# Down-projection of a gated MLP with tokens on partitions: weights as the moving operand, two Strassen lots of 16 K tiles, and the final norm along the free axis

## The chip, the cores and the metric

The kernel runs on one core of one Trainium2 chip. Its time is the device time of one execution in microseconds (us). Before the change three runs took 2834.66, 2835.13 and 2835.55 us.

## The reference

One layer of a decoder on x of 512 tokens by 2048 features (`S`, `D`), all in float32. Six vectors of 2048 (shift, scale and gate, twice) come from a conditioning vector c. The change touches the end:

```python
mod = silu(c) @ w_ada + b_ada
sh1, sc1, gt1, sh2, sc2, gt2 = split(mod, 6)
h = rmsnorm(x, g_mix) * (1 + sc1) + sh1
x = x + (1 + gt1) * mixer(h, positions, w_in, w_a, w_b, w_o)
h = rmsnorm(x, g_ffn) * (1 + sc2) + sh2
u = conv_b + causal depthwise convolution of width 3 of (h @ w_up)
a, b = split(u, 2)
x = x + (1 + gt2) * ((silu(a) * b) @ w_down)          # w_down: 5632 x 2048
out = rmsnorm(x, g_final)
```

`rmsnorm(x, g)` divides each token by the root of its mean square over the 2048 features and multiplies by g.

## The kernel before, in words

Features lie on partitions and the 512 tokens along the free axis nearly everywhere: an activation is a list of tiles of 128 features by 512 tokens, and 2048 features are 16 of them (`KT`), 5632 are 44 (`NJ`). A K tile is 128 rows of a weight matrix.

**Three products for one.** Every float32 operand is split into a high and a low part that TensorE takes in its fp32r format (`parts` and `prep` for weights: `wh` on ACT, L132, `wl` on DVE, L134; `split` for activations: L161 and L163). `mm3` (L140 to L144) issues three matmuls: high by high (L142), high by low (L143), low by high (L144). The operand named first stands in the array, the second moves.

**Strassen units.** `unit` multiplies n K-tile pairs of a weight matrix by an activation with seven products of half size instead of eight. Its matmuls move half of the tokens, 256 columns. DVE forms sums of weight quarters (L232, L236, L270, L274) and of the products (L240, L272, L273, L276, L278). A unit with 16 K tiles makes 168 matmuls and two output tiles. w_x (32 units, 64 output tiles, loop at L635), w_o (8 units, L1047) and w_up use it. A unit calls `between` twice, after its second and fourth product, and there other work is put into the queues. In w_x that is the next step of `beside()` (rope tables, rope of the indexer's operands), and one `ada` half at the second call (`some_ada`).

**Ada halves.** `ada_half` (L295) loads 128 rows by 1024 columns of w_ada (512 KB) and lets DVE multiply by silu(c) and sum along the row (L298). The numbers t = 0 to 95 stand for the 96 tiles of the six vectors. The gate of the MLP is t = 80 to 95.

**Down-projection (from L1168).** `yd` in DRAM holds silu(a) * b, two K tiles to a tile. `group` runs six plain K tiles over all 16 output tiles: 288 matmuls of 512 columns, sums to `sumd` in DRAM. Then eight Strassen units over the next 16 K tiles (loop at L1229), each with 168 matmuls of 256 columns; the sums are added to `sumd` and saved to `sume`. Then `group` runs the last 22 K tiles: for each output tile 66 matmuls of 512 columns, and in the last tile 132 of 256 columns, one half of the tokens after the other. With each output tile come two `ada` halves (`prepare`, L1246), the load of x1 (the residual, kept in `x1d`), the load of `sume`, and on DVE the sum with them (L1243, L1244). ACT squares the tile (L984) and POOL adds up the squares (L986).

**Final norm.** The squares lie along partitions, so `rms` (L338) sums them with matmuls against ones, takes root and reciprocal (L348, L349), and spreads the result over the partitions with two more matmuls (L355). DVE (L1287) and POOL (L1285) multiply the 16 tiles by it and g_final, and eight transfers of 512 KB bring them out, L1289. The second half of the tokens does this after the last matmul.

**w_o.** Each of the first seven units adds x (`residual`), saves x1 to `x1d`, squares it and adds the squares up with an accumulate DMA on POOL (L1062).

**Order and queues.** A tile scheduler places the instructions by priority; within an engine they run in the written-out row, and a waiting instruction holds all behind it on its engine. Loads of weights, of `ada` and the outputs go through SP's queue, loads and saves of activations and all accumulate DMAs through POOL's. Tiles with a tag share a small set of buffers (`raw` has 8, `wh` and `wl` 3 each).

Of the kernel before, what the change touches and what calls it, by code (L numbers as in the profile page):

```python
# [10 lines left out]
F32 = mybir.dt.float32  # L11
# [7 lines left out]
P = 128  # L19
# [12 lines left out]
FIRST = 6  # L32
MID = 16
LAST = NJ - FIRST - MID
# [41 lines left out]
def block_kernel(ctx: ExitStack, tc: tile.TileContext, A: dict, out: bass.AP):  # L76
# [36 lines left out]
    vec = sb.tile([P, 96 + 3 * KT], F32, tag="vec", name="vec")  # L113
    nc.scalar.dma_start(vec, A["vecs"])
    b_ada = vec[:, :96]
    g_mix, g_ffn, g_fin = (vec[:, 96 + i * KT : 96 + (i + 1) * KT] for i in range(3))
# [168 lines left out]

    def c_silu():
        cb = []
        for half in range(2):
            c = t2k("raw", 8, w=1024)
            nc.sync.dma_start(c, A["c"][:, half * 1024 : (half + 1) * 1024].to_broadcast([P, 1024]))  # L290
            act(c, c, AF.Silu)
            cb.append(c)
        return cb
# [324 lines left out]
    ada_left = [(t, half) for t in range(32, 80) for half in range(2)]  # L618
# [359 lines left out]
    x1d = [dr.tile([P, S], F32, tag=f"x1d{j}", name=f"x1d{j}") for j in range(KT)]  # L978
    x1 = []

    def squares(x, j, done):

        sq = t2k("T", 2) if j == 0 else t2k("w", 2)
        act(sq, x, AF.Square)  # L984
        if 0 < j < KT - 1:
            nc.gpsimd.tensor_tensor(done[0], done[0], sq, ALU.add)  # L986
        else:
            done.append(sq)

    def between(i, *pins):  # L990
        with behind(*pins):
            if i:
                some_ada()
# [53 lines left out]
    for u in range(KT // 2):  # L1047
# [6 lines left out]
        for i, c in enumerate(unit(A["w_o"][u], f, between, late)):  # L1054
            j = 2 * u + i
            if not late:
                residual(c, j, xr[i])
                nc.gpsimd.dma_start(x1d[j], c)
                sq = t2k("T", 2) if j == 0 else both[:, i * S : (i + 1) * S]
# [5 lines left out]
        if u == KT // 2 - 2:  # L1065
            some_ada(len(ada_left))
            ada_end(48, 80)
# [94 lines left out]
    for j in range(NU, NJ):  # L1162
        if j < 2 * NU:
            finish(j - NU, *ups[2 * (j - NU) : 2 * (j - NU) + 2])
        finish(j, *unit(A["w_up"][j - NU], f))


    def group(src, first, n, stop, done):  # L1168

        chunks = [(c, min(8, n - c)) for c in range(0, n, 8)]  # L1170

        def weights(j):
            return [prep(src[j, :, c * P : (c + m) * P], m * P) for c, m in chunks]

        y = []
        ps = acc(), att()
        for c, m in chunks:
            w = [prep(src[j, :, c * P : (c + m) * P], m * P) for j in range(2)]
            for k in range(c, c + m, 2):
                at = yd[(first + k) // 2]  # L1180
# [201 lines left out]
```

## Time and profile before

| what | before |
|---|---|
| three runs, median | 2835.13 us |
| profiled execution, time | 2834.82 us |
| profiled execution, span | 2832.7 us |
| mean granted clock of TensorE, share of full | 0.996 |
| PE busy | 2785.6 us, 98% |
| DVE, ACT, POOL busy | 84%, 49%, 9% |
| moved by DMA | 510.81 MB |

The span runs from the first instruction to the last; the time includes what lies around it. Busy times are sums of instructions that did work, waits not included. The stage in question is the last sixth, from 2338.8 us. The rows that go with it stand below, ahead of the prediction.

### The profile page before, as it was taken

The numbers are of one execution on the slowest core, as the hardware profiler recorded it, in microseconds if no ns is written. First come the engines' busy times: TensorE is split into PE (matmuls) and PEld (weight loads), VectorE is DVE, ScalarE is ACT, GpSimd is POOL, SyncE is SP. The second block draws the span as 40 slices with busy tenths as digits, with TensorE's granted clock in tenths as the row PEclk, the third lists the DMA queues.
The fourth block names the chain that finished last, engine by engine and source line by source line (L and its number), as shares of the span: only waits on it lengthen the run. The fifth ranks groups of instructions, "written<-read, shape, count | busy, mean of one in ns | idle before, by whom it ended". The sixth has DMA issues, their size and how long they took to land.

```text
span 2832.7 us, 49071 instructions
## 1 busy us (share of the span) xinstructions
PE 2785.6 (98%) x19562; PEld 2589.8 (91%) x19562; DVE 2387.5 (84%) x3446; ACT 1383.6 (49%) x1951; POOL 261.5 (9%) x452
## 2 busy tenths in 40 slices
PE   9999999999999999999999999999999999999997
PEld 6779999999998768889999999999999998998886
DVE  8979888988897899788888988888888887886554
ACT  5544444455556665434466554545454555444221
POOL 0100000000002111111110000000000001010111
PEclk9999999999999999999999999999999999999999
DMA  9964456555566458766552333333333346448663
GB/s 358 335 224 148 159 180 206 203 172 177 182 210 213 153 169 304 251 203 206 181 188 101 125 114 123 114 126 110 127 109 127 109 138 232 162 150 287 218 191 128
DMA packets 151880, 510.81 MB, mean 180 GB/s; under 512 B 19474, under 2 KB 23954, under 8 KB 151652
## 3 DMA queue, kind: packets, MB, share of 16 engines
q1 hardware_dynamic: 116836, 397.47, 41.9%
q0 software_dynamic: 34368, 109.83, 11.3%
q8 instruction: 153, 2.51, 0.4%
q14 instruction: 75, 0.61, 0.1%
q10 hardware_dynamic: 448, 0.39, 0.0%
HBM read 443.74 MB, written 60.46 MB: 178 GB/s over the span
## 4 chain that ended last, share of the span: by engine, by line
PE 82%; DVE 9%; issue 5%; DMA 2%; ACT 1%; POOL 0%; DVEq 0%; ACTq 0%; POOLq 0%
PE acc L144 13%; PE acc L142 13%; PE acc L143 13%; PE att L144 13%; PE att L142 13%; PE att L143 13%; DVE raw L298 2%; DVE wl L134 2%; DVE F L163 1%; DMA raw<-in_w_va 1%; PE acc L714 1%; PE acc L808 1%; ACT wh L132 1%; PE acc L776 0%; PE outs L914 0%
## 5 line engine op out<-in xcount | busy, mean ns | idle before, releaser
L132 ACT ACTIVATE wh<-raw 128x1024 fp32r<-128x1024 f32 (+2 forms) x787 | 820.3, 1044 | 1164.0 <-PE acc L143 299.0
L134 DVE TENSOR_TENSOR wl<-raw,wh 128x1024 fp32r<-128x1024 f32 (+2 forms) x787 | 943.3, 1201 | 151.6 <-ACT wh L132 140.8
L142 PE MATMUL acc<-F,wh 128*128 128x256 f32 (+1 forms) x2996 | 890.5, 299 | 6.8 <-ACT F L161 5.0
L144 PE MATMUL acc<-F,wl 128*128 128x256 f32 (+1 forms) x2996 | 894.6, 299 | 1.7 <-DVE wl L134 1.6
L143 PE MATMUL acc<-F,wh 128*128 128x256 f32 (+1 forms) x2996 | 895.5, 299 | 0.1
L144 PE MATMUL att<-F,wl 128*128 128x256 f32 (+1 forms) x2858 | 852.3, 298 | 3.0 <-DVE wl L134 3.0
L143 PE MATMUL att<-F,wh 128*128 128x256 f32 (+1 forms) x2858 | 852.7, 298 | 1.2 <-DVE F L163 1.2
L142 PE MATMUL att<-F,wh 128*128 128x256 f32 (+1 forms) x2858 | 848.8, 299 | 5.0 <-ACT wh L132 4.6
L142 PEld LDWEIGHTS acc<-F,wh 128*128 128x128 f32 x2996 | 572.9, 191 | 27.6 <-ACT F L161 6.8
L143 PEld LDWEIGHTS acc<-F,wh 128*128 128x128 f32 x2996 | 573.3, 191 | 20.4 <-DVE F L163 2.3
L144 PEld LDWEIGHTS acc<-F,wl 128*128 128x128 f32 x2996 | 573.1, 191 | 20.0 <-DVE wl L134 2.5
L142 PEld LDWEIGHTS att<-F,wh 128*128 128x128 f32 x2858 | 547.6, 192 | 23.5 <-ACT wh L132 5.8
L143 PEld LDWEIGHTS att<-F,wh 128*128 128x128 f32 x2858 | 547.8, 192 | 19.9 <-DVE F L163 4.3
L144 PEld LDWEIGHTS att<-F,wl 128*128 128x128 f32 x2858 | 547.4, 192 | 19.8 <-DVE wl L134 4.5
L298 DVE SCALAR_TENSOR_TENSOR raw<-raw,raw 128x1024 f32<-128x1024 f32 x186 | 227.0, 1228 | 71.1 <-DMA raw<-in_w_ada 63.1
L232 DVE TENSOR_TENSOR raw<-raw,raw 128x1024 f32<-128x1024 f32 x89 | 108.5, 1219 | 13.3 <-DMA raw<-in_w_x 9.1
L236 DVE TENSOR_TENSOR raw<-raw,raw 128x1024 f32<-128x1024 f32 x89 | 108.7, 1221 | 1.4
L274 DVE TENSOR_TENSOR raw<-raw,raw 128x1024 f32<-128x1024 f32 x88 | 107.5, 1221 | 1.5
L270 DVE TENSOR_TENSOR raw<-raw,raw 128x1024 f32<-128x1024 f32 x88 | 107.1, 1217 | 0.1
L1088 POOL DMA_DIRECT2D yd<-w x44 | 23.8, 540 | 871.7 <-DVE w L1087 830.0
L142 PE MATMUL att<-wh,F 128*128 128x512 f32 x192 | 78.3, 408 | 0.0
L144 PE MATMUL att<-wh,F 128*128 128x512 f32 x192 | 75.3, 392 | 0.0
(301 smaller groups left out, 2664.0 us busy)
## 6 DMA issues: line engine op xcount, KB each, us to landing
raw<-in_w_ada SPq DMA_DIRECT2D x186, 512.0 KB, 4.9
raw<-in_w_up SPq DMA_DIRECT2D x164, 512.0 KB, 3.3
raw<-in_w_x SPq DMA_DIRECT2D x128, 512.0 KB, 4.0
raw<-in_w_down SPq DMA_DIRECT2D x64, 512.0 KB, 4.4
xd<-F POOLq DMA_DIRECT2D x64, 256.0 KB, 3.0
F<-xd POOLq DMA_DIRECT2D x64, 256.0 KB, 4.5
raw<-in_w_o SPq DMA_DIRECT2D x32, 512.0 KB, 4.0
raw<-in_w_down SPq DMA_DIRECT2D x32, 384.0 KB, 4.1
```

The source lines that it names most:

```text
L132: act(wh, raw, AF.Copy)
L134: tt(wl, raw, wh.bitcast(F32), ALU.subtract)
L142: mm(ps, ah, bh, start=first, stop=False, skip_group_check=not check)
L143: mm(ps, ah, bl, start=False, stop=False, skip_group_check=not check)
L144: return mm(ps, al, bh, start=False, stop=last, skip_group_check=not check)
L163: tt(lo, src, hi.bitcast(F32), ALU.subtract)
L232: last_v = tt(s, a21, a22, ALU.add)
L236: tt(s, s, a11, ALU.subtract)
L270: tt(a11, a11, a21, ALU.subtract)
L274: tt(a12, a12, s, ALU.subtract)
L298: stt(raw, raw, 1.0, cb[half], ALU.mult, ALU.mult, accum_out=macc[:, t, half : half + 1])
L714: mm(dots[:, :W], both[:, b * P : (b + 1) * P], kiR[i][:, :W], start=i == 0, stop=i == 1)
```

## The change

**Layout.** In the down-projection, tokens now lie on partitions and the output features along the free axis. The split activation (128 K rows by 128 tokens) stands in the array, and weights move, 512 output features at a time. There are 16 output blocks (t, b): 128 tokens by 512 features. The 44 K tiles become 6 plain, 16 Strassen, 2 plain, 16 Strassen, 4 plain (`AT`). A Strassen lot pairs the K tiles, token halves and feature halves; it runs in two halves v of 1024 features, each four groups of K tiles times seven products of 12 matmuls, 336 of 512 columns.

**Sums.** Plain and first-lot blocks go to `sumd` in DRAM, by accumulate DMAs on POOL (`add_to`). In the second lot `base_of` takes each block, adds `sumd` to it by an accumulate DMA into SBUF, multiplies by the gate row on DVE (L1307 of the new code), and adds x1, token-major, by another accumulate DMA. The last four K tiles are multiplied by the gate row and added to that.

**Moved.** x1 is turned on PE in the w_o stage (`turn`, 4 transposes per tile, an ACT copy and a save to `x1t`; the last tiles within the first w_up units). The 32 `ada` halves of the gate go into units 16 to 31 of w_x, two more per unit. The gate row is saved to DRAM as one row, 2,048 elements of 4 bytes each, and loaded as a broadcast.

**Removed.** The reload of x1, the matmuls of the final `rms`, POOL's sums of squares, and `c_silu`. The final norm squares along the free axis with a sum in the same ACT instruction, has four groups of tokens, and 16 output transfers of 256 KB. The output has shape (4, 128, 2048) on the device.

```diff
+D0, D1, D2 = 6, 2, 4
+AT = [0, D0, D0 + MID, D0 + MID + D1, D0 + 2 * MID + D1]
...
-    ada_left = [(t, half) for t in range(32, 80) for half in range(2)]
+    ada_left = [(t, half) for t in range(32, 96) for half in range(2)]
...
             with behind(*pins):
                 next(work)
-                if i:
+                if i or u >= 16:
+                    some_ada()
+                if i and u >= 16:
                     some_ada()
...
+    def turn():
+
+        if to_turn:
+            j, x = to_turn.pop(0)
+            ps = outs()
+            for b in range(NQB):
+                nc.tensor.transpose(ps[:, b * P : (b + 1) * P], x[:, b * P : (b + 1) * P], ident)
+            o = slot()
+            act(o, ps, AF.Copy)
+            save(x1t[:, :, j * P : (j + 1) * P], o.rearrange("p (b f) -> p b f", b=NQB))
...
+            save(gate_row.rearrange("o (t p) -> p (o t)", p=P), gates)
...
+    add_to = lambda o, i: nc.gpsimd.dma_start(o, i, accum_op=ALU.add)
...
+                for i in range(2):
+                    k = 2 * c + i
+                    for t in range(NQB):
+                        mm3(ps[t], cols(y[k], t), cols(w, i, S), k == 0, k == n - 1)
...
+    def strassen_down(v, src, f, done, step=lambda i: None):
+
+        r1, rb = [att() for _ in range(2)], [att() for _ in range(2)]
+        ra, rc = [acc() for _ in range(2)], [acc(), outs()]
+        groups = range(len(f) // 2)
+
+        def product(ps, raw, name, g, first):
+            w = parts(raw)
+            for k in range(2):
+                for i in range(2):
+                    mm3(ps[i], cols(f[2 * g + k][name], i), cols(w, k, S), first and g + k == 0,
+                        g == groups[-1] and k == 1, check=False)
+
+        kept = []
+        for g in groups:
+            a11, a21, a22 = (load(src[g, q]) for q in (0, 2, 3))
+            product(r1, a11, "B11", g, True)
+            tt(a21, a11, a21, ALU.subtract)
+            product(ra, a21, "T3", g, True)
+            tt(a22, a22, a21, ALU.subtract)
+            product(rb, a22, "T2", g, True)
+            tt(a11, a22, a11, ALU.add)
+            product(rc, a11, "T1", g, True)
+            kept.append(a22)
+            step(g)
...
+        for i in range(2):
+            c22.append(slot())
+            tt(c22[i], rc[i], x[i], ALU.add)
+        for i in range(2):
+            tt(c22[i], c22[i], e3[i], ALU.add)
+            done((2 + i, 2 * v + 1), c22[i])
+        for g in groups:
+            a12, a22 = (load(src[g, q]) for q in (1, 3))
+            product(r1, a12, "B21", g, False)
+            product(ra, a22, "T4", g, False)
+            tt(a12, a12, kept[g], ALU.subtract)
+            product(rc, a12, "B22", g, False)
+            step(len(groups) + g)
...
+    def base_of(tb, c):
+        t, b = tb
+        add_to(c, sumd[tb])
+        tt(c, c, row[b], ALU.mult)
+        add_to(c, x1t[:, t, b * S : (b + 1) * S])
+        if b < 2:
+            save(sumd[tb], c)
+        else:
+            base[tb] = c
...
+    strassen_down(0, A["w_down3"][0], f2, base_of)
+    gate_rows(1)
...
+    strassen_down(1, A["w_down3"][1], f2, base_of, last_operands)
...
+            for k in range(D2):
+                mm3(o, cols(y[k], t), last_w[b, k], k == 0, k == D2 - 1)
+            if b < 2:
+                base[t, b] = fetch(sumd[t, b])
+            x = slot()
+            tt(x, o, row[b], ALU.mult)
+            tt(x, x, base[t, b], ALU.add)
+            act(t2k("ta", 2), x, AF.Square, accum_out=s[:, b : b + 1])
+            xs.append(x)
...
+        for b, x in enumerate(xs):
+            stt(x, x, r[:, 3:], g_row[b], ALU.mult, ALU.mult)
+            nc.sync.dma_start(out[t][:, b * S : (b + 1) * S], x)
```

Here is how that stands in DVE's row at the places that the prediction speaks of. In the new code most lines are numbered by one more (L135 is `wl`) or by eight less (L290 is the `ada` half). First, DVE in the second half of w_x, before the change, around the one `ada` half of a unit:

```order
L240 TENSOR_TENSOR sp_6661<-att_6556,ta_6594 128x256
L298 SCALAR_TENSOR_TENSOR raw_6700,macc<-raw_6700,raw_86 128x1024
L583 TENSOR_TENSOR soft_6392<-soft_6392,T_5973 128x512
L134 TENSOR_TENSOR wl_6737<-raw_6564,wh_6735 128x1024
L585 TENSOR_TENSOR w_6391<-soft_6392 128x512
L134 TENSOR_TENSOR wl_6766<-raw_6562,wh_6764 128x1024
L232 TENSOR_TENSOR raw_6838<-raw_6802,raw_6804 128x1024
L272 TENSOR_TENSOR sp_6661<-att_6556,ta_6594 128x256
L273 TENSOR_TENSOR F_6692<-sp_6661,ta_6594 128x256
```

And with the change, in a unit of the second half of w_x:

```order
L135 TENSOR_TENSOR wl_6237<-raw_6087,wh_6235 128x1024
L241 TENSOR_TENSOR sp_6190<-att_6085,ta_6123 128x256
L569 TENSOR_TENSOR soft_5982<-w_5981,T_5975 128x512
L290 SCALAR_TENSOR_TENSOR raw_6228,macc<-raw_6228,raw_79 128x1024
L290 SCALAR_TENSOR_TENSOR raw_6231,macc<-raw_6231,raw_86 128x1024
L135 TENSOR_TENSOR wl_6268<-raw_6093,wh_6266 128x1024
L135 TENSOR_TENSOR wl_6297<-raw_6091,wh_6295 128x1024
L233 TENSOR_TENSOR raw_6369<-raw_6333,raw_6335 128x1024
```

Two `ada` halves stand one behind the other ahead of `wl`; the next one, at the first call of the unit that follows, stands eleven rows behind them.

Second, DVE in a Strassen unit of the down-projection before, where a block (F) is finished and the old sum (w) added, L1234, between weights of the next unit:

```order
L272 TENSOR_TENSOR sp_27610<-att_27510,ta_27548 128x256
L273 TENSOR_TENSOR F_27641<-sp_27610,ta_27548 128x256
L134 TENSOR_TENSOR wl_27754<-raw_27744,wh_27752 128x1024
L276 TENSOR_TENSOR F_27640<-att_27511,sp_27610 128x256
L1234 TENSOR_TENSOR F_27640<-F_27640,w_27733 128x512
L134 TENSOR_TENSOR wl_27786<-raw_27782,wh_27784 128x1024
L236 TENSOR_TENSOR raw_27782<-raw_27782,raw_27744 128x1024
L278 TENSOR_TENSOR F_27641<-att_27510,ta_27548 128x256
L270 TENSOR_TENSOR raw_27744<-raw_27744,raw_27746 128x1024
L1234 TENSOR_TENSOR F_27641<-F_27641,w_27737 128x512
L134 TENSOR_TENSOR wl_27816<-raw_27782,wh_27814 128x1024
```

DVE in the middle of v = 0 of the second lot, with the change (L1250 and L1252 finish a block, L1258 is an operand sum, L1307 the product with the gate row, kept in `soft`):

```order
L1250 TENSOR_TENSOR F_28573<-acc_28267,T_28565 128x512
L1250 TENSOR_TENSOR F_28575<-outs_28268,T_28571 128x512
L1252 TENSOR_TENSOR F_28573<-F_28573,w_28563 128x512
L1252 TENSOR_TENSOR F_28575<-F_28575,w_28569 128x512
L1258 TENSOR_TENSOR raw_28587<-raw_28587,raw_28273 128x1024
L1307 TENSOR_TENSOR F_28573<-F_28573,soft_28259 128x512
L135 TENSOR_TENSOR wl_28626<-raw_28587,wh_28624 128x1024
L1307 TENSOR_TENSOR F_28575<-F_28575,soft_28259 128x512
L135 TENSOR_TENSOR wl_28646<-raw_28640,wh_28644 128x1024
L135 TENSOR_TENSOR wl_28662<-raw_28642,wh_28660 128x1024
```

L1307, which needs a block after its accumulate DMA, now stands ahead of the `wl` of the third product that follows.

Third, DVE at the change from v = 0 to v = 1 of the second lot:

```order
L1271 TENSOR_TENSOR F_28823<-acc_28267,T_28565 128x512
L1271 TENSOR_TENSOR F_28829<-outs_28268,T_28571 128x512
L135 TENSOR_TENSOR wl_28870<-raw_28847,wh_28868 128x1024
L1307 TENSOR_TENSOR F_28811<-F_28811,soft_28259 128x512
L135 TENSOR_TENSOR wl_28887<-raw_28849,wh_28885 128x1024
L1307 TENSOR_TENSOR F_28817<-F_28817,soft_28259 128x512
L1236 TENSOR_TENSOR raw_28845<-raw_28849,raw_28845 128x1024
L1307 TENSOR_TENSOR F_28823<-F_28823,soft_28259 128x512
L1232 TENSOR_TENSOR raw_28993<-raw_28991,raw_28993 128x1024
L1307 TENSOR_TENSOR F_28829<-F_28829,soft_28259 128x512
L135 TENSOR_TENSOR wl_28904<-raw_28845,wh_28902 128x1024
```

Here four such products lie between the last block sums and the `wl` of the fourth product of v = 1.

## Rows read from the trace of the kernel before

**Rows 1.** The page, busy us, share of the span and instructions.

```profile
PE 2785.6 (98%) x19562; PEld 2589.8 (91%) x19562; DVE 2387.5 (84%) x3446; ACT 1383.6 (49%) x1951; POOL 261.5 (9%) x452
```

**Rows 2.** Windows of the down-projection: us, busy of PE, PEld, DVE, ACT, POOL; clock, DMA.

```profile
2338.00:2404.00 66.00, 66.00 (x297) 54.79 (x296) 50.00 (x90) 35.84 (x63) 9.71 (x18) 1.00 0.69 232
2404.00:2566.00 162.00, 161.90 (x1348) 161.62 (x1347) 134.12 (x154) 71.24 (x91) 16.41 (x31) 1.00 0.50 167
2566.00:2805.00 239.00, 235.07 (x1057) 195.41 (x1056) 136.85 (x194) 69.19 (x86) 31.24 (x33) 0.99 0.64 209
2805.00:2833.00 28.00, 11.06 (x88) 10.43 (x86) 11.82 (x32) 3.41 (x7) 7.53 (x11) 0.75 0.46 154
```

**Rows 3.** Windows, PE alone: us, busy (count), clock, DMA share, GB/s.

```profile
868.00:886.00 18.00, 18.00 (x81) 1.00 0.76 254
2340.00:2400.00 60.00, 60.00 (x266) 1.00 0.72 244
2410.00:2560.00 150.00, 149.90 (x1250) 1.00 0.49 164
```

**Rows 4.** Timeline of PE: start, us, line, then idle before and releaser.

```profile
2577.10 0.39 PE L144 MATMUL acc<-F,wl 128*128 128x512 f32 x1
2581.42 0.80 PE L142 MATMUL att<-F,wh 128*128 128x512 f32 x1 [3.93 <-ACT wh L132]
```

**Rows 5.** Window behind that wait; the clock is the 0.50.

```profile
2580.30:2587.10 6.80, 5.68 (x13) 4.51 (x14) 5.80 (x8) 5.92 (x10) 0.00 (x0) 0.50 0.81 261
```

**Rows 6.** Timeline: first and last matmul of the stage, last products of the norm.

```profile
2338.82 0.40 PE L142 MATMUL acc<-F,wh 128*128 128x512 f32 x1
...
2814.13 0.28 PE L144 MATMUL acc<-F,wl 128*128 128x256 f32 x1
...
2819.81 4.40 DVE L1287 SCALAR_TENSOR_TENSOR raw<-F,vec,att 128x256 f32<-128x256 f32 x11 [1.29 <-ACT ta L1280]
```

**Rows 7.** Timeline of DVE in w_x, instructions of 1024 columns back to back.

```profile
837.55 1.22 DVE L298 SCALAR_TENSOR_TENSOR raw<-raw,raw 128x1024 f32<-128x1024 f32 x1
...
838.70 2.36 DVE L134 TENSOR_TENSOR wl<-raw,wh 128x1024 fp32r<-128x1024 f32 x2
```

**Rows 8.** Accumulate DMAs of w_o, one line: issue ns and landing us, min/median/max.

```profile
L1062 POOL DMA_DIRECT2D T<-soft x13: 887/913/947, 1299.1 to 1419.5; - x13
...
DMA to landing us min/median/max: 3.3/4.1/5.6
```

**Rows 9.** Groups by form from 2280: count, busy us, mean ns, idle before.

```profile
L1244 DVE SCALAR_TENSOR_TENSOR F<-ta,mod,F 128x512 f32<-128x512 f32 x15 | 11.1, 746 | 0.0
...
L984 ACT ACTIVATE w<-F 128x512 f32<-128x512 f32 x14 | 8.9, 633 | 33.9 <-DVE F L1244 33.9
...
L1243 DVE TENSOR_TENSOR ta<-acc,ta 128x512 f32<-128x512 f32 x8 | 5.5, 690 | 8.8 <-PE acc L144 8.8
...
L348 ACT ACTIVATE r<-att,eps 128x2 f32<-128x2 f32 x2 | 0.5, 262 | 0.9 <-PE att L344 0.9
```

**Rows 10.** DMA issues: count, KB each, median us to landing.

```profile
w<-in_x POOLq DMA_DIRECT2D x16, 256.0 KB, 4.2
...
out_x<-raw SPq DMA_DIRECT2D x8, 512.0 KB, 4.0
```

**Rows 11.** Windows of w_x, columns as in rows 2.

```profile
551.00:872.00 321.00, 320.80 (x2653) 319.65 (x2653) 279.22 (x338) 174.82 (x235) 28.61 (x53) 1.00 0.57 187
832.00:852.00 20.00, 20.00 (x169) 20.00 (x168) 19.19 (x24) 10.05 (x14) 1.47 (x3) 1.00 0.69 226
233.20:253.40 20.20, 19.69 (x162) 19.27 (x161) 20.16 (x32) 8.12 (x10) 1.08 (x2) 1.00 0.51 170
```

**Rows 12.** Timeline of PE around four transposes (L904).

```profile
1109.60 0.48 PE L144 MATMUL att<-F,wl 128*128 128x512 f32 x1
...
1109.92 0.60 PE L904 MATMUL acc<-const,soft 128*128 128x128 f32 x4
...
1110.27 0.47 PE L142 MATMUL att<-F,wh 128*128 128x512 f32 x1
```

More of the change, by code (lines that the diff above doesn't have):

```diff
@@ L978, in block_kernel @@
     x1d = [dr.tile([P, S], F32, tag=f"x1d{j}", name=f"x1d{j}") for j in range(KT)]
+    x1t = dr.tile([P, NQB, D], F32, tag="x1t", name="x1t")
+    gate_row = dr.tile([1, D], F32, tag="gate", name="gate")
     x1 = []
[L981 to L988, printed above, removed]
+    to_turn = []
+    def turn():
[7 more added lines that the diff above has]
+            save(x1t[:, :, j * P : (j + 1) * P], o.rearrange("p (b f) -> p b f", b=NQB))
     def between(i, *pins):
+        turn()
         with behind(*pins):
@@ L1205, in block_kernel @@
-    sumd = dram("sumd", KT)
-    f = [{} for _ in range(MID // 2)]
-    def pair_forms():
+        elif j < 2 * NU + 2:
+            x = t2k("T", 2)
+            save(x, x1d[KT - 2 + j - 2 * NU])
+            to_turn.append((KT - 2 + j - 2 * NU, x))
+        finish(j, *unit(A["w_up"][j - NU], f, lambda *_: turn()))
+    TB = [(t, b) for b in range(4) for t in range(NQB)]
+    sumd = {tb: dr.tile([P, S], F32, tag=f"sumd{tb}", name="sumd{}{}".format(*tb)) for tb in TB}
+    add_to = lambda o, i: nc.gpsimd.dma_start(o, i, accum_op=ALU.add)
@@ L1246, in prepare @@
-    def prepare(j):
-        if not cb:
-            cb.extend(c_silu())
-        x1.append(slot())
-        nc.sync.dma_start(x1[j], x1d[j])
-        t = 80 + j
-        for half in range(2):
-            ada_half(cb, t, half)
-        ada_end(t, t + 1)
-        ts(mod[:, t : t + 1], mod[:, t : t + 1], 1.0, None, ALU.add)
-    def done(j, ps):
-        prepare(j)
-        add_to(j, ps)
-        squares(x1[j], j, sums)
-        if j % 3 == 1:
-            act(x1[j], x1[j], AF.Copy, scale=g_fin[:, j : j + 1])
@@ new lines, in second_sum, with gate_rows @@
+    def second_sum(tb, c):
+        keep(tb, c)
+        if tb[0] == NQB - 1:
+            run(forms2)
+    plain_down(A["w_down2"], [], range(AT[2] // 2, AT[3] // 2), second_sum)
+    run(forms2, MID)
+    base = {}
+    row = {}
+    def base_of(tb, c):
[4 more added lines that the diff above has]
+        if b < 2:
+            save(sumd[tb], c)
+        else:
+            base[tb] = c
+    def gate_rows(v):
+        r = sb.tile([P, 10 * P], F32, tag="soft", name=nm("soft"))
+        save(r[:, :1024], gate_row[:, v * 1024 : (v + 1) * 1024].to_broadcast([P, 1024]))
+        for i in range(2):
+            row[2 * v + i] = r[:, i * S : (i + 1) * S]
@@ new lines, in block_kernel, with last_operands, last_weights @@
+    gate_rows(0)
+    strassen_down(0, A["w_down3"][0], f2, base_of)
+    gate_rows(1)
+    y, last_w = [], {}
+    def last_operands(i):
+        if i == 3:
+            for p in range(AT[4] // 2, NJ // 2):
+                y.extend(two_tiles(p))
+        elif i > 3:
+            last_weights(i - 4)
+    def last_weights(b):
+        for c in range(D2 // 2):
+            raw = load(A["w_down4"][b, c])
+            for i in range(2):
+                last_w[b, 2 * c + i] = split(raw[:, i * S : (i + 1) * S])
```

197 lines of the change are left out of this document (92 added, 105 removed).

## The prediction, on record before the changed kernel ran

> **What bounds the kernel now.** I read the page's busy line first. TensorE (PE) is busy for 2785.6 of 2832.7 us, VectorE (DVE) for 84%, ScalarE (ACT) for 49%, GpSimd (POOL) for 9% [rows 1]. So the time is PE's, and an edit counts by what it takes from PE's stream or makes PE wait for. DVE, at 84%, is the engine that could take over. Second, the four stages of the down-projection by windows [rows 2]: in the first three PE is busy for all but 4 us; the fourth, the last 28 us, is mostly other engines' work. Third, PE's cadence in three quiet stretches [rows 3]: 1,250 matmuls of 256 columns take 150 us, 120.0 ns each; 266 of 512 columns, features on partitions, take 60 us; 81 of 512 columns with the weights moving (in the values' projection) take 18 us. A count includes the one or two that straddle an edge; with 264.5 whole ones the 60 us make 226.8 ns for 512 columns. I take that, and no difference for which operand moves. 512 columns thus cost 1.89 times 256, not 2.
>
> Fourth, the one large wait of the stage: between two matmuls that start at 2577.10 and 2581.42 PE stands for 3.93 us, put down to ACT's `wh`, which itself stood behind a load of `yd` [rows 4]; behind it the granted clock is 0.50, that is 1.2 GHz, for 6.8 us [rows 5]. Last, the end: the last matmul of the main stream starts at 2814.13, the norm's last pieces begin on DVE at 2819.81 and end 4.40 us later, and from there it is 8.5 us to the end of the span (the last output transfers and the closing) [rows 6].
>
> The base of the sum is the profiled run: span 2832.7, time 2834.8, which is 0.3 us under the median of 2835.1. The stage runs from 2338.8 to the span's end, 493.9 us: 475.4 of main stream and 18.5 of tail [rows 6].
>
> **The change part by part.**
>
> *Matmuls of the down-projection.* Before: 1,344 of 256 columns in eight Strassen units, 288 + 990 of 512 columns, and 132 of 256 in the last tile; at the cadences that is 177.1 + 289.9 = 467 us, and 8 us of the 475.4 are the stall, its half clock and the ends. After: 12 plain tiles make 576 and two Strassen lots 2 x 672 = 1,344, all of 512 columns: 1,920 x 0.2268 = **435.5 us**. The gain of 39.9 has two sources: sixteen more K tiles get seven products for eight, and no matmul is of 256 columns.
>
> The row with the weights moving settles the price by itself. The Trainium skill (TensorE: Matmul & The Clock Gate, "Back-to-back issue gap") gives a warm spacing of N/2.4 GHz plus 2.5 ns, 109 ns for 256 columns and 216 for 512. That makes two short ones as dear as a long one within 1%, and by it the main stream would fall by only about 22 us, an estimate from that page. The trace disagrees: 120.0 and 226.8.
>
> *PE waits in the Strassen lots.* Each v half is 336 matmuls or 76.2 us; DVE has there 28 `wl` and 16 operand sums of 1024 columns at about 1.15 us [rows 7] and ten sums of 512, some 57 us. In lot 1 the finished blocks leave on accumulate DMAs for which nobody waits, and DVE has the next two products' `wl` ready first: 0. In lot 2 each block is added to by a DMA, then DVE multiplies it by the gate row (L1307 of the new code), and that product stands in DVE's row ahead of `wl`. The nearest row for such a DMA is the 13 accumulates of the w_o stage: 0.89 to 0.95 us on POOL and 3.3 to 5.6 to land [rows 8], so about 5 us from block to product. In the middle of v = 0 PE has two products (24 matmuls, 5.4 us) in hand, while DVE needs 2.0 for the sums of the block, 5.0 for the DMA, 0.7 for the product and 1.2 for the `wl`, 8.9: 3 us of wait. In the middle of v = 1 the same, a little less: 2.5. Between the two halves six such blocks follow each other and three `wl` stand between their products: 6 (4 to 9). At the two plain tiles between the lots, where DVE also forms the lot's sums: 1.5 (0 to 4). Sum **13** (5 to 22). The stall of before cost 3.4 us more by its half clock [rows 5]; one such in four waits: **4** (0 to 8).
>
> *Tail.* The last matmul 0.3; product with the gate row and sum with the base, 0.69 each; square 0.63; root 0.26, with tiny sums, reciprocal and hand-overs about 1; four products of 512 at 0.75 or a little less back to back, 2.8 [rows 9]; then what stood behind the last piece before, 8.5 [rows 6], less 1 because an output is 256 KB and not 512 KB, whose transfer takes 4.0 [rows 10]. That is 13.6. The base blocks come through two accumulate DMAs each, so DVE starts the first norm groups late while PE runs the 192 last matmuls (43.5 us): +2. **15.6** (13.6 to 21), against 18.5 of before.
>
> *Gate halves.* 32 `ada` halves, each a load of 512 KB and 1.15 us of DVE from start to start (837.55 to 838.70) [rows 7], leave the last stage, where they were DVE's and not PE's time, and go to units 16 to 31 of w_x. There DVE is busy for 279.2 of 321 us [rows 11]; 36.8 more make 316, 98%. Per unit of 20.2 us: the ones with one `ada` so far have room. The last three units already carry two more (the `soft` ones): 19.19 of 20.00 us [rows 11], with 2.3 more 21.5 against 20.2, or 1.3 us over, three times: **4** (0 to 12; the upper end is every one of the 16 units losing 0.75: an early unit of w_x, with DVE at 20.16 of 20.20, let PE fall to 19.69 [rows 11]).
>
> *Transposes of x1.* 64 on PE, four to a tile, between matmuls of the w_o stage. The trace has the same form in the sparse heads: four start at 1109.92 and the next matmul starts at 1110.27, and the 512-column matmul ahead takes 0.32 instead of 0.23 [rows 12]: 0.44 per tile, 16 tiles: **7.0**. The copies are ACT's, which is half idle; the saves to `x1t` are POOL's, which is at 9%. The cover is that both have room; without it `x1d` and the next unit's `x` come later, and a unit there would lose what that transfer takes, 4.2 us, once [rows 10].
>
> *At nothing:* the end without rms matmuls and `rstd` spread is in the tail; the squares that POOL summed vanish with idle time on POOL; the loads of partial sums become accumulate DMAs on the same queue.
>
> Sum: after 435.5 + 13 + 4 + 15.6 = 468.1; against 493.9 that is -25.8; + 7.0 + 4 = **-14.8**. 2834.8 - 14.8 = **2820.0**.
>
> **The rivals.**
>
> *A, clean.* DVE runs further ahead than I count, the lot-2 waits come to 5, no clock drop, w_x free, tail 13.6: 435.5 + 5 + 13.6 + 7.0 = 461.1, -32.8: 2802. For it: PE's waits of before sum to few us in all though DVE is at 84%. Against: the order puts L1307 ahead of `wl`, and the DMA has a price. I take 2802 to 2811.
>
> *B, same sign gone.* All lot-2 waits and the tail at their upper ends: 22 + 8 + 21 in place of 32.6, +18.4: 2838. For it: the landing time of an accumulate into DRAM has no row, and POOL, which issues all of them, is in order. Against: none of the 13 that the trace has is over 5.6 [rows 8].
>
> *C, slower: units 16 to 31 of w_x become DVE's.* Each unit has 17.45 us of DVE and gets 2.3; PE's next product needs a `wl` at its place in DVE's row, and an `ada` that waits for its load holds all that follow. It needs 0.4 us per unit over my count to show, and from 1.6 us per unit (25.6 in place of 4, with the rest as forecast) the kernel comes within the measurement's bound of before and passes it; at 1.9 to 2.0 the time is 2847. For it: 98% in order leaves no room, and eight `raw` buffers have more claimants. Against: the last units already ran with three `ada` and PE at 20.00 of 20.00 [rows 11].
>
> *D, 512 columns with the weights moving cost two of 256,* 240 ns: +25 us: 2845. Only the 81 in 18 us speak [rows 3], and against it. The page named above comes near this rule.
>
> **How the numbers follow.** A difference of 0.2% (5.7 us) is about what this kernel's runs can tell from none: faster is below 2829.5, slower above 2840.8. Chances: forecast (2812 to 2829) 0.49, A 0.22, B (2830 to 2840) 0.15, C 0.11, D 0.02, the rest lower. Faster 0.72, same 0.15, slower 0.13. The range leaves out half of C and D above and a tenth of A below: 2804 to 2842.
>
> **What would show it.** The windows of the Strassen lots: 76.2 us of PE per v half plus the waits; waits of PE on `wl` behind L1307 of 2 to 5 us at three places of lot 2 and none in lot 1. If those are under 1 us, A. The w_x window: 321 us plus 3 to 5; more than 8 is C. Transposes: 16 gaps of 0.44. Tail: 15 to 18 us behind the last matmul. The prediction is wrong if the cadence of the new matmuls isn't 227 ns, if PE waits in lot 1, or if an accumulate DMA lands much later than 5 us.

## The result and the profile after

The changed kernel took 2861.3 us (median of 4 runs, 2858.76 to 2864.51) against 2834.99 before: a ratio of 1.0093, 95% interval 1.0076 to 1.0111. It is slower by 26 us. The forecast was 2820, and 2842 was the upper end of the range. The profiled execution took 2859.5 us, span 2857.7, that is 25.0 more span than before. Where these lie, by the starts of the same instructions in the two traces (a save of the attention branch writes `yad`, one of w_up writes `yd`):

| stretch | forecast | measured |
|---|---|---|
| w_x, up to the attention branch's last save (987.42 before, 1008.90 after) | +4 | +21.5 |
| from there to the first matmul of the down-projection (2338.82, 2365.74) | +7.0 | +5.4 |
| down-projection, first to last matmul (475.3, 472.2) | -22.9 | -3.1 |
| behind the last matmul (18.6, 19.8) | -2.9 | +1.2 |
| sum | -14.8 | +25.0 |

Two terms carry the miss: the row of w_x by 17.5 and the waits of the down-projection by 20; the tail adds 4, and the transposes give back 1.6. The matmuls themselves came as priced. The page's busy line, and one window of the first lot (us, PE busy and count, clock, DMA share, GB/s):

```profile
PE 2780.4 (97%) x18772; PEld 2546.5 (89%) x18772; DVE 2458.7 (86%) x3525; ACT 1432.9 (50%) x2031; POOL 287.3 (10%) x482
```

```profile
2431.00:2508.00 77.00, 77.00 (x340) 1.00 0.59 177
```

PE, beside [rows 1], is busy for 5 us less in a span that is 25 us longer; DVE for 71 more. With one or two straddlers off the 340, the new matmuls, 512 columns with the weights moving, follow each other at 227 ns, as in [rows 3]. 1,920 of them are 435.5 us, so 36.7 of the 472.2 are waits and what hangs on them. Rival D is out. The spacing of 216 ns that the Trainium skill gives for a matmul by itself (TensorE: Matmul & The Clock Gate, "Back-to-back issue gap") is not met here either.

**w_x.** Windows of its first and its second half (us; busy of PE, PEld, DVE, ACT, POOL; clock, DMA share, GB/s), and what DVE waited for in the second (us in total, times, longest):

```profile
230.00:551.00 321.00, 319.53 (x2633) 316.61 (x2632) 285.72 (x411) 137.79 (x173) 20.49 (x38) 1.00 0.56 184
551.00:890.00 339.00, 328.35 (x2640) 323.32 (x2639) 310.69 (x400) 174.66 (x232) 28.52 (x53) 0.98 0.68 224
```

```profile
DVE raw L233 <- DMA raw<-in_w_x: 10.9, 11, 2.2
DVE w L600 <- DMA w<-qid: 10.7, 3, 3.9
DVE sp L241 <- PE acc L145: 1.8, 2, 0.9
```

The first half is as before. In the second DVE works for 310.7 us, 31 more than in [rows 11], and still stands idle for 28, most of it for weights to form an operand sum from (L233) and for an operand of the indexer (L600). PE is busy for 328 of 339 us; its waits there add up to 10.4 us, none over 1.4. Of these, 8.1 us lie in four places, three of them behind the three waits of DVE for `qid`, of which this is the first, and one at 828:

```profile
628.02 0.69 DVE L600 TENSOR_TENSOR w<-w,w 128x512 f32<-128x512 f32 x1 [3.95 <-DMA w<-qid]
```

Before the change DVE waited for the same three operands, 6.3 us in all, and PE waited 0.2 us in the whole half. Behind three of the four places the granted clock is 0.50 for 3.4 us:

```profile
635.80:639.20 3.40, 3.40 (x18) 3.40 (x18) 2.65 (x3) 0.87 (x3) 0.00 (x0) 0.50 0.50 155
```

That does not set the price: in six profiles with the same 32 halves in this place, the second half has one to four such stretches and takes 340.9 to 343.9 us, 341.9 with one and 341.9 with four.

By the saves of w_x's output tiles (`xd`) the second half takes 343.9 us here against 326.5 before, 17.4 of the 21.5 in the table. The other 4.1 lie in the attention branch behind it, which takes 119.4 us for 115.3. That goes with the gate halves too: it takes 118.5 to 119.4 in the six profiles that have them in the second half of w_x, and 115.3 to 116.4 in the eight others.

**The second lot.** What PE waited for in the whole down-projection; then DVE's row (start, us, instruction, idle before and releaser) and PE's at the change from v = 0 to v = 1:

```profile
PE acc L144 <- DVE wl L135: 7.3, 4, 3.0
PE att L144 <- DVE wl L135: 5.7, 4, 2.3
PE acc L143 <- ACT F L411: 3.8, 1, 3.8
PE acc L143 <- ACT wh L133: 2.7, 3, 1.5
PE att L143 <- ACT F L162: 1.7, 1, 1.7
```

```profile
2700.52 0.69 DVE L1307 TENSOR_TENSOR F<-F,soft 128x512 f32<-128x512 f32 x1 [3.60 <-DMA F<-sumd]
...
2704.14 1.21 DVE L135 TENSOR_TENSOR wl<-raw,wh 128x1024 fp32r<-128x1024 f32 x1
2707.99 0.69 DVE L1307 TENSOR_TENSOR F<-F,soft 128x512 f32<-128x512 f32 x1 [2.63 <-DMA F<-sumd]
2708.60 1.22 DVE L135 TENSOR_TENSOR wl<-raw,wh 128x1024 fp32r<-128x1024 f32 x1
2712.03 0.69 DVE L1307 TENSOR_TENSOR F<-F,soft 128x512 f32<-128x512 f32 x1 [2.21 <-DMA F<-sumd]
```

```profile
2701.96 0.47 PE L143 MATMUL acc<-wh,F 128*128 128x512 f32 x1 [0.52 <-DVE F L1267]
2705.41 0.80 PE L144 MATMUL acc<-wl,F 128*128 128x512 f32 x1 [2.98 <-DVE wl L135]
2706.00 0.63 PE L145 MATMUL acc<-wh,F 128*128 128x512 f32 x1
```

Each L1307 waits for its accumulate DMA, and the `wl` that stands behind it in the row comes late; PE then waits for that `wl`. Behind such a wait the matmuls start 0.43 us apart and the granted clock is 0.50, the lower of the two levels (1.2 GHz). There were four such stretches in this stage. Ahead of three of them stands one wait of 2.3 to 3.8 us, ahead of the one at 2719 four shorter ones of 3.5 us together. The windows of three of them:

```profile
2616.00:2622.00 6.00, 5.59 (x13) 4.18 (x13) 4.25 (x8) 4.02 (x9) 3.47 (x4) 0.50 0.88 168
2705.40:2710.90 5.50, 5.49 (x13) 4.38 (x14) 1.83 (x2) 0.00 (x0) 2.54 (x5) 0.50 1.05 200
2719.00:2724.80 5.80, 5.76 (x14) 4.50 (x15) 4.53 (x4) 1.06 (x1) 2.28 (x4) 0.50 0.98 217
```

With 3.2 us more at 2769 they are 20.5 us at half clock, 10 us lost, where [rows 5] had one of 6.8. In all, what starts of matmuls lie apart beyond 0.227 us (called gaps below) adds up, place by place and with the half clock, to 13.7 us around the two plain tiles between the lots (2583 to 2636), 3.1 in the middle of v = 0, 14.1 at the change to v = 1 and 5.7 in the middle of v = 1.

Around the plain tiles it begins with DVE: it stood 9.2 us for the weights of the second lot's first operand sum. SP issued their load only at 2587.33, when DVE had freed its `raw` buffer with the last instruction ahead of that wait. Behind it forms of the activation came late, and ACT, whose row waits for these, emptied a PSUM bank late for PE (the 3.8 us at L411):

```profile
2586.12 1.53 SPq L126 DMA_DIRECT2D raw<-in_w_down  x2
2596.53 1.23 DVE L1232 TENSOR_TENSOR raw<-raw,raw 128x1024 f32<-128x1024 f32 x1 [9.23 <-DMA raw<-in_w_down]
2611.64 0.63 ACT L162 ACTIVATE F<-sp 128x512 fp32r<-128x512 f32 x1 [4.94 <-DVE sp L176]
```

The accumulate DMAs themselves, all those issued by `add_to` (issue ns min/median/max, then us to landing min/median/max), beside [rows 8]:

```profile
L1179 POOL DMA_DIRECT2D sumd<-F x32: 852/1044/1854, 2476.6 to 2618.3; - x32
L1179 POOL DMA_DIRECT2D F<-sumd x16: 842/967/1621, 2664.9 to 2802.8; - x16
...
DMA to landing us min/median/max: 3.8/6.7/12.4
```

The 12.4 is one into `sumd`, for which DVE does not wait. For the second lot's own (window 2660:2820) the last line is:

```profile
DMA to landing us min/median/max: 3.8/6.0/8.7
```

**The tail.** DVE and POOL at the last blocks:

```profile
2810.87 0.69 DVE L1307 TENSOR_TENSOR F<-F,soft 128x512 f32<-128x512 f32 x1 [8.93 <-DMA F<-sumd]
...
2821.11 2.50 DVE L1364 TENSOR_TENSOR F<-F,F 128x512 f32<-128x512 f32 x4 [6.93 <-DMA F<-sumd]
```

```profile
2803.30 1.78 POOL L1343 DMA_DIRECT2D F<-gate  x2
2804.41 1.73 POOL L1343 DMA_DIRECT2D F<-in_g_row  x2
2811.86 0.88 POOL L1179 DMA_DIRECT2D F<-x1t  x1 [5.71 <-DVE F L1307]
2812.42 1.43 POOL L1343 DMA_DIRECT2D F<-in_g_row  x2
2813.49 1.96 POOL L646 DMA_DIRECT2D F<-sumd  x3
```

POOL's row holds an accumulate that waits for DVE, behind it two row loads, and behind these the loads of the bases that the first norm group needs. DVE stands for 8.9 and 6.9 us while PE runs the last matmuls, and is still 16 us from its end when PE stops at 2838.

### The profile page after: what moved, and what is told of

Read it like the earlier page. It is cut to its first block, busy times and chain, and to the rows that moved or that the text cites. A ratio compares the mean times of both kernels' runs of the same rounds, so it can differ in the third digit from the quotient of the medians.

```text
span 2857.7 us, 47675 instructions
## 1 busy us (share of the span) xinstructions
PE 2780.4 (97%) x18772; PEld 2546.5 (89%) x18772; DVE 2458.7 (86%) x3525; ACT 1432.9 (50%) x2031; POOL 287.3 (10%) x482
## 4 chain that ended last, share of the span: by engine, by line
PE 74%; DVE 12%; DMA 6%; issue 6%; ACT 2%; POOL 1%; DVEq 0%; ACTq 0%; POOLq 0%; SPq 0%
PE att L145 11%; PE att L144 11%; PE att L143 11%; PE acc L145 11%; PE acc L143 11%; PE acc L144 11%; DVE wl L135 3%; DVE raw L290 2%; DVE F L164 1%; DMA F<-sumd 1%; DMA raw<-in_w_x 1%; DMA raw<-in_w_va 1%; ACT wh L133 1%; DMA raw<-in_w_down 1%; PE acc L802 1%
## 5 line engine op out<-in xcount | busy, mean ns | idle before, releaser
L135 DVE TENSOR_TENSOR wl<-raw,wh 128x1024 fp32r<-128x1024 f32 (+2 forms) x795 | 958.2, 1211 | 137.2 <-ACT wh L133 130.2
L143 PE MATMUL acc<-F,wh 128*128 128x256 f32 (+1 forms) x2504 | 729.4, 294 | 9.8 <-ACT F L162 5.0
L145 PE MATMUL acc<-F,wl 128*128 128x256 f32 (+1 forms) x2504 | 733.2, 293 | 4.0 <-DVE wl L135 3.9
L144 PE MATMUL acc<-F,wh 128*128 128x256 f32 (+1 forms) x2504 | 733.1, 293 | 0.1
L145 PE MATMUL att<-F,wl 128*128 128x256 f32 (+1 forms) x2432 | 710.9, 293 | 4.8 <-DVE wl L135 4.8
L144 PE MATMUL att<-F,wh 128*128 128x256 f32 (+1 forms) x2432 | 711.0, 292 | 1.2 <-DVE F L164 1.2
L143 PE MATMUL att<-F,wh 128*128 128x256 f32 (+1 forms) x2432 | 707.8, 294 | 3.5 <-ACT wh L133 2.0
L143 PEld LDWEIGHTS acc<-F,wh 128*128 128x128 f32 x2504 | 480.6, 192 | 23.1 <-ACT F L162 6.8
L144 PEld LDWEIGHTS acc<-F,wh 128*128 128x128 f32 x2504 | 480.9, 192 | 10.9 <-DVE F L164 1.6
L143 PEld LDWEIGHTS att<-F,wh 128*128 128x128 f32 x2432 | 467.2, 192 | 14.5 <-ACT wh L133 3.6
L144 PEld LDWEIGHTS att<-F,wh 128*128 128x128 f32 x2432 | 467.2, 192 | 11.9 <-DVE F L164 4.3
L290 DVE SCALAR_TENSOR_TENSOR raw<-raw,raw 128x1024 f32<-128x1024 f32 x186 | 224.4, 1218 | 9.4 <-ACT raw L323 8.1
L144 PE MATMUL att<-wl,F 128*128 128x512 f32 x448 | 177.0, 395 | 5.7 <-DVE wl L135 5.7
L143 PE MATMUL att<-wh,F 128*128 128x512 f32 x448 | 177.7, 398 | 2.0 <-ACT F L162 1.7
L145 PE MATMUL att<-wh,F 128*128 128x512 f32 x448 | 175.9, 393 | 0.0
L143 PE MATMUL acc<-wh,F 128*128 128x512 f32 x288 | 114.5, 398 | 7.1 <-ACT F L411 3.8
L233 DVE TENSOR_TENSOR raw<-raw,raw 128x1024 f32<-128x1024 f32 x81 | 98.6, 1218 | 20.3 <-DMA raw<-in_w_x 15.8
L145 PE MATMUL acc<-wh,F 128*128 128x512 f32 x288 | 114.6, 398 | 0.0
```

Source lines behind the costliest of these rows:

```text
L135: tt(wl, raw, wh.bitcast(F32), ALU.subtract)
L143: mm(ps, ah, bh, start=first, stop=False, skip_group_check=not check)
L144: mm(ps, ah, bl, start=False, stop=False, skip_group_check=not check)
L145: return mm(ps, al, bh, start=False, stop=last, skip_group_check=not check)
L233: last_v = tt(s, a21, a22, ALU.add)
L290: stt(raw, raw, 1.0, cb[half], ALU.mult, ALU.mult, accum_out=macc[:, t, half : half + 1])
```

## Experiments

### One part alone, on the kernel before: gate halves in w_x

```diff
-                if i:
+                if i or u >= 16:
+                    some_ada()
+                if i and u >= 16:
                     some_ada()
```

with the loads and products of the gate halves gone from `prepare`.

> The kernel before with one part of the change alone: the 32 gate halves in units 16 to 31 of w_x, nothing left out. Theory 1: w_x takes 16 to 20 us more, and the last stage, without 16 MB of loads, loses its stall of 4 us with half clock: 2835 + 18 - 4 to 7 = 2845 to 2850. My forecast's price: +4 - 5: 2834.

2854.15 us against 2835.95, ratio 1.0066 (1.0046 to 1.0086): 18 more by this part alone (two runs, 2851.9 and 2856.4). In the profile 16.7 lie up to w_x's last save and 3.4 in the attention branch, and the stages behind these take 2.5 less:

```profile
551.00:890.00 339.00, 327.34 (x2651) 321.89 (x2650) 311.46 (x401) 174.86 (x234) 28.55 (x53) 0.99 0.68 226
```

The window is that of the changed kernel. The last stage did not get shorter without its 16 MB of loads (473.8 us from its last `yd` save to the last matmul, those of the final norm included; 474.3 before). The guess that the wait of [rows 4] would go was wrong. Without it the expected 16 to 20 us in w_x make 2851 to 2855:

```profile
PE att L142 <- ACT wh L132: 4.0, 1, 4.0
```

### The gate left out, and the same 32 halves spread over w_x

> The changed kernel without the 32 gate halves in units 16 to 31 of w_x (the gate row is made from another part of the modulation vector, so the MLP's gate is left out; every later step stays). Theory 1, DVE with 98% of w_x's second half and PE behind it: w_x ends 17 to 21 us earlier than in the changed kernel, as in the kernel before, and the time falls from 2861 to 2840 to 2844. Rival, that the transfers of the gate halves or something else of the stage cost the time and DVE is only a symptom: the same fall, but w_x's DVE idle time with it unchanged; a third, my forecast, that they cost 4 us: 2857.

2847.79 in one run, 13.5 less than the changed kernel, and outside all the ranges expected. The second half of w_x took 333.5 us by the saves of its output tiles, against 343.9 and 326.5 before: one load of an `ada` half for the `soft` buffer came 6.2 us late there, and PE waited 4.1 for it.

```profile
838.96 1.19 POOL L1069 DMA_DIRECT2D gate<-mod  x1 [3.01 <-DVE raw L275]
853.02 1.23 DVE L290 SCALAR_TENSOR_TENSOR soft<-soft,raw 128x1024 f32<-128x1024 f32 x1 [6.20 <-DMA soft<-in_w_ada]
```

The edit itself brought this about, as far as the trace tells: its gate row is made of numbers that are ready earlier, so the save of that row, at 1372 in the changed kernel, fell into w_x. It landed after 13.0 us, and the three loads of 512 KB issued 2.6 to 6.2 us behind it took 11.5 to 13.0. So this run gives the sign and not the size; the one on w_up gives the size.

```diff
-                if i or u >= 16:
-                    some_ada()
-                if i and u >= 16:
-                    some_ada()
+                some_ada()
```

> The changed kernel, nothing left out, with the same 32 gate halves spread over all 32 units of w_x, one more in each, in place of two more in each of the last 16. Theory 1 (DVE's row full: 98% of the second half's time with its waits on top): DVE stays under 95% in both halves, and w_x loses 2 to 8 us in place of 17 to 21: 2844 to 2852. Rival, each half costs PE a fixed 0.5 us wherever it stands in w_x: 2859 to 2864 as before this edit.

2850.02 in one run, inside the expected range. But w_x lost some 12 us and not 2 to 8; the rest of the gain lies behind w_x. Its two halves:

```profile
230.00:551.00 321.00, 315.54 (x2592) 311.82 (x2591) 298.01 (x441) 133.39 (x169) 20.50 (x38) 1.00 0.64 205
551.00:880.00 329.00, 322.53 (x2652) 320.13 (x2651) 294.57 (x367) 174.95 (x234) 26.54 (x50) 0.99 0.64 205
```

By the saves, the second half took 336.6 us with 16 halves more; the five runs that had none more, and nothing left out, took 324 to 329. That is about 9.5 us, 0.6 for each, and 17.4 for the 32 of the changed kernel is 0.54 for each. In the first half, which took 316.7 us against 313.3 to 315.2 in those five and 312.7 in the changed kernel, the other 16 cost 3 to 4 us, some 0.2 each. So, by this one run, the price is neither one figure for all of w_x nor a threshold at a full DVE: in the second half half of an `ada`'s 1.15 us reaches PE even with DVE busy for 90% of the time.

### The gate halves in w_up

One half per unit in 32 of the 41 w_up units, with silu(c) loaded anew as the kernel before did for the last stage.

```diff
+    def beside_up(i, *pins):
+        turn()
+        if i and j >= 2 * NU and late_ada:
...
+            with behind(*pins):
+                ada_half(late_cb, *late_ada.pop(0))
...
-        finish(j, *unit(A["w_up"][j - NU], f, lambda *_: turn()))
+        finish(j, *unit(A["w_up"][j - NU], f, beside_up))
```

> The changed kernel with nothing left out: the 32 gate halves go to 32 of the w_up units, one per unit, in place of two more per unit in w_x. Theory 1: w_x gets back 17 to 21 us, and w_up, whose units take 20.2 us with DVE at about 85%, loses 0 to 4: 2841 to 2846. If it is the load that costs wherever it stands (512 KB more per unit, eight raw buffers): w_up loses what w_x gained, 2855 or more.

2842.22 (2840.07 to 2845.83, 10 runs), 19 less than the changed kernel; ratio to before 1.0027 (1.0018 to 1.0036). The second half of w_x took 327.9 us, and from the branch's last save to the last `yd` save it is 1363.8 us against 1362.8: w_up takes the same 32 loads and products for 1 us. A window of 600 us of w_up in this run:

```profile
1700.00:2300.00 600.00, 599.54 (x4997) 599.37 (x4996) 559.66 (x682) 299.55 (x387) 17.99 (x32) 1.00 0.44 143
```

DVE is busy for 93% there, more than in w_x with the same halves, and PE for 599.5 of 600. Neither the load nor the product costs by itself, nor a busy DVE; the place does. The place differs in more than one way. In this window DVE waits for loads 19.1 us in 600, never over 2.2, against 22.3 in 339 and up to 3.9 in w_x, and the DMA engines are busy for 0.44 of the time against 0.68.

### The second lot without its accumulate DMAs, and with L1307 later in the row

Left out in the first: the additions of `sumd` and x1 to the second lot's blocks.

> The changed kernel with the accumulate DMAs of the second lot's blocks left out (neither the partial sum nor x1 is added; product with the gate row and everything else stay). Theory 2, that DVE's product with the gate row waits in its row for an accumulate DMA and holds the weights behind it: PE's waits from 2640 to 2773 fall from about 28 us with their half clock to under 4, the last matmul comes 24 to 28 us earlier, and the tail, whose first groups waited for those DMAs, 2 to 4 more: 2831 to 2836. Rival, that loads of weights come late in the second lot whatever DVE waits for: under 10 us.

2829.6 in one run, 31.7 less. From the last `yd` save to the last matmul it takes 445.5 us for 466.2, less of a gain than the 24 to 28 expected; the gaps of the second lot are down to 1.6 us, and the tail to 10.2, more than expected. The 14 us around the plain tiles stay.

Nothing left out in the second: the product is pinned behind the `wl` of a later product, 5 to 15 DVE instructions on.

```diff
-        tt(c, c, row[b], ALU.mult)
-        add_to(c, x1t[:, t, b * S : (b + 1) * S])
...
+        waiting.append((tb, c, row[b]))
...
+    def settle(n):
+        for _ in range(min(n, len(waiting))):
+            (t, b), c, r = waiting.pop(0)
+            with behind(pins["wl"]):
+                tt(c, c, r, ALU.mult)
+            add_to(c, x1t[:, t, b * S : (b + 1) * S])
```

> The changed kernel with nothing left out: the product with the gate row of the second lot stands five to fifteen DVE instructions later in the row, behind weights that the next products need. Theory 2: most of what leaving the DMAs out brings, -18 to -26 us, 2835 to 2843. Rival (late loads, or POOL's row as the bound): under 10 us, 2851 or more.

2837.12 (2832.87 to 2839.7, 10 runs), 24 less. DVE in the middle of v = 0 (L1315 is the product):

```profile
2663.28 1.22 DVE L1258 TENSOR_TENSOR raw<-raw,raw 128x1024 f32<-128x1024 f32 x1
2665.70 3.50 DVE L135 TENSOR_TENSOR wl<-raw,wh 128x1024 fp32r<-128x1024 f32 x3 [1.21 <-ACT wh L133]
...
2672.68 1.29 DVE L1315 TENSOR_TENSOR F<-F,soft 128x512 f32<-128x512 f32 x2
```

Both products now find their blocks landed; no idle stands before them. The accumulates of `sumd`, issued as before, cost PE nothing there: it was the place of the product in DVE's row. The gaps of the second lot are 5 us, and the tail 15.3.

### Both edits, the rows through SP, and the order between the lots

> Both edits at once, nothing left out: gate halves in w_up, and the product with the gate row later in DVE's row. If the two causes are separate the gains add: -19 and -24 from 2861 make 2818 (2815 to 2821), faster than the kernel before by 14 to 19. If a shared resource (DVE, POOL's queue) is behind both, less: 2825 or more.

2815.75 (2815.41 to 2816.59), ratio to before 0.9933 (0.9916 to 0.9951). The two gains add, 45.6 for 19 and 24.

In the next, the rows and the bases of the first 1024 columns come through SP into `raw` buffers, in place of POOL's queue.

```diff
-    for b in range(2):
-        row[b] = row_of(gate_row, b)
-    g_row = [row_of(A["g_row"], b) for b in range(4)]
+    def wide_row(src, v):
+        r = t2k("raw", 8, w=1024)
+        nc.sync.dma_start(r, src[:, v * 1024 : (v + 1) * 1024].to_broadcast([P, 1024]))
+        return [r[:, i * S : (i + 1) * S] for i in range(2)]
```

> As the run before it, and the gate and g rows and the bases of the first 1024 columns for the final norm come through SP's queue into weight buffers during the second lot, in place of POOL's queue behind the last accumulate DMAs. Theory 3, that the tail is long because these loads queue behind the accumulates on POOL: the tail behind the last matmul falls from 15 to 11 or 12 us, 2814. Rival, DVE's own work sets the tail: within 1 us of the run before.

2812.67 (2810.07 to 2815.11), ratio 0.9922 (0.9906 to 0.9938). The tail fell from 14.2 to 10.3 us; of the time, 3 of these 4 show, and the two intervals overlap. DVE meets the last matmul's block 0.44 us after its last work:

```profile
2800.91 0.69 DVE L1399 TENSOR_TENSOR F<-outs,soft 128x512 f32<-128x512 f32 x1 [0.44 <-PE outs L145]
```

The next two make DVE finish the activation's forms ahead of the second lot's first operand sums, all of them (first run) or those of six pairs (second).

> As the run before it, and in the two plain tiles between the lots DVE makes all forms of the activation ahead of the second lot's operand sums, in place of waiting for that lot's weights in between. Theory 4, that DVE stands 9 + 3 + 2 us for these loads ahead of work that PE needs: PE's loss from 2580 to 2636, 13 us with its half clock, falls to 4 to 7, 2806 to 2810. Rival, DVE has too much work there for the 22 us of PE: no gain, 2812 or more.

2817.22 (2812.89 to 2819.38): no gain. The wait moved, as the rival had it, into one wait of PE for a weight split:

```profile
PE acc L143 <- ACT wh L133: 10.9, 1, 10.9
```

> As the run with both edits and the rows through SP, and the second lot's operand sums wait for the forms of six of the eight pairs only, in place of all. In the run that waited for all, PE stood 10.9 us for a weight split behind them; with six, PE's loss in this region is to be 8 to 12 us in place of 13: 2808 to 2813. If no order of DVE helps because the loads land late (7 to 12 us beside the accumulates): 2813 to 2817.

2811.03 (2810.37 to 2813.14) against 2835.95 before, ratio 0.9916 (0.9900 to 0.9933), 25 us faster than the kernel before. The gaps around the plain tiles fell from 13.4 to 10.4 us; its interval overlaps that of the run with the rows alone, so the last step is seen in the trace and not in the time.

### Between the lots without the accumulates, and w_o without the transposes

> The changed kernel without the 16 accumulate DMAs of the two plain tiles between the lots (those two K tiles are left out of the result; their matmuls stay). Theory 5, that the weights of the second lot land late there because these accumulates fill the DMA engines (busy share 1.10): DVE's wait of 9.2 us for them falls to under 4 and PE's loss from 2580 to 2636 from 13 us to 6 or less; 2851 to 2855. Rival, that their buffers come free late: within 3 us of the changed kernel.

2854.53 in one run, 6.8 less. The gaps around the plain tiles are 8.6 us for 13.7. But DVE's first wait there stays:

```profile
DVE raw L1232 <- DMA raw<-in_w_down: 9.4, 1, 9.4
```

Its load, issued at 2586.3, landed 9.3 us later beside six accumulates of the first lot's last blocks, which were kept and took 7 to 12 us themselves. So the theory holds in part: only the later waits were due to the 16 that were left out, and of the 6.8 us some 5 are theirs. The rival, a buffer that comes free late, has its part in the first wait: here as in the changed kernel SP issues this load just as DVE begins to wait for it. The loads of `in_w_down` issued from 2560 to 2576 landed in 4.3 to 5.6 us in the two traces, so about half of the 9.4 would stay without any accumulates beside it (an estimate).

> The changed kernel without the 64 transposes of x1 (the copy and the save to x1t take the tile as it stands, so x1 enters the output in the wrong order). By the prediction's price, 0.44 us per tile, 7.0 less than the changed kernel from the end of w_x to the down-projection. If the copies and saves beside them cost something too, less than the 5 to 7 us by which these stages were longer is given back: 2 to 4.

2852.52 in one run, of which 5.9 us lie where the transposes were (1356.9 from the branch's last save to the last `yd` save, against 1362.8, and 1357.2 before); the rest is elsewhere and within what single runs of this kernel differ. The copies and saves cost nothing that shows; the transposes 0.37 us per tile.

## Why the prediction was wrong

**The cadence and the count: right.** 1,920 matmuls at 227 ns, and no wait of PE in lot 1, as forecast. The 39.9 us that the sum put down to two sources hold a third: 8 of them are the wait of [rows 4], its half clock and the ends; the cadences alone make 31.5.

**Transposes: right in kind, a little dear.** 5.4 to 5.9 us for 7.0.

**Gate halves, +4 forecast, 17.4 in w_x and 21.5 with the branch behind it: the step "36.8 more make 316, 98%" failed.** It added DVE's work to the window and took the rest as free. But DVE's idle in w_x is not spare: it stands for loads and for PE within each unit. The sum left no time for its waits on `raw<-in_w_x` and `w<-qid` (21.6 us after). The price by units, which only charged the last three, rested on one unit that had run with three halves. Rival C named the mechanism and held it for 0.11, with a point of 1.6 us per unit from which it would alone decide; measured was 1.1 to 1.3. That is 17 to 21 us in all, over the 8 that were to be its sign. The `ada` part alone on the kernel before settles it: +18 in time where the sum had +4.

What makes half of each product reach PE there and none of it in w_up, with DVE at 92 and 93%, was not told apart by a run. Three things stay open: the `raw` buffers, for which SP's queue waits until DVE has freed them; the fuller DMA engines; and the indexer's work on DVE with its loads, which only w_x has beside its products. The trace of the changed kernel speaks for the last, as most of PE's waits stand where it does; but with the halves spread, DVE waited 0.2 us for `qid` and the second half still lost 9.5.

**Waits in the Strassen lots, 13 forecast, about 26 in waits and 10 in half clock.** The mechanism in lot 2 was right, and moving one instruction confirmed it. Its sizes were nearly so: without the half clock its three places cost 3.1, 8.4 and 4.1 us for 3, 6 and 2.5 (the terms given for the first make 3.5). The landing of an accumulate was bounded by [rows 8], 5.6 at most; those rows go one at a time into one SBUF tile, and here two to six follow each other: 6.0 median in lot 2, 8.7 at most, for "5.0 for the DMA". The term that failed is the plain tiles between the lots: 1.5 forecast, 10.7 in waits and 13.7 with the half clock. The estimate counted DVE's work there. It left out that the second lot's first operand sums stand in DVE's row ahead of forms that PE needs, and wait 9 us for a load that is issued late and lands slowly beside the accumulates. Three more stretches of half clock followed than the one I carried over from before: 10 us for 4.

**Tail, 15.6 forecast, 19.8.** The backlog of "+2" was the step: the last base and the rows queue on POOL one behind the other. Taking them off POOL gave 10.3, under the 13.6 that I had as the lower end (whose terms add up to 13.9).

**The upper ends.** Three of the four unknown terms lay past their own upper ends (w_x 17.4 to 21.5 past 12; waits 26 past 22; clock 10 past 8) and the tail near it (19.8 of 21), all in one direction, since in all of them, as I read the traces, a row of DVE or POOL is worked in order while a transfer lands late. The range treated them as if one case at a time would go wrong.

## What to carry to other kernels

On an engine that works its row in order, idle time is not free room: before adding work to it, look at what its idle ends with, and put the work in the stage where a trial costs nothing. Look also at when the buffer comes free from which a load is issued: a load that starts as its reader begins to wait costs a whole landing. An instruction that waits for a DMA belongs so far down the row that the longest landing, not the median of the quietest rows, is over before it; moving it 5 to 15 places gave 24 us here. Price each transfer by rows with the same number in flight.

## What the hardware showed

An accumulate DMA of 256 KB landed in 3.8 to 12.4 us where several followed each other, and its issue took POOL 0.84 to 1.85 us; plain saves of that size issue in 0.54. The gate row, saved as 2,048 elements of 4 bytes, was slow in every run whose trace has its landing (KB, median us to landing in the changed kernel):

```profile
gate<-mod POOLq DMA_DIRECT2D x1, 8.0 KB, 12.3
```

In the five runs that have it in w_up, with little else beside it, it landed in 10.0 to 10.4 us. Loads of w_up's weights, 512 KB each, have a median of 3.9 to 4.0 us there; the one in flight ahead of this save landed in 4.2 to 4.4, the one issued 5 us behind it in 8.8 to 9.4.

The Trainium skill says that a strided last dimension lowers to one descriptor per element (DMA: Bandwidth & Descriptors, "Rules for kernel authors"); the 10 to 13 us of all these runs are in keeping with it, but no view here counts the descriptors. In the changed kernel it was hidden: it landed at 1384.4, and the first load of that row was issued at 1450.5. Rows loaded as broadcasts landed in 7.9 to 8.5 us. Plain loads of 256 KB had medians from 3.1 to 9.0 in the same trace, so whether a broadcast costs more is not shown.
